# Five projections instead of three in the first pass of a streaming-encoder layer, with the input's squares on ScalarE

## The chip, the cores and the metric

The kernel runs on one core of a Trainium2 chip. The metric is device time in microseconds (us) of one execution. A profiled execution of each kernel gives the trace: what every engine did and when, in us from the first instruction.

## What is computed

One layer of a hybrid encoder over 272 tokens (16 learned ones and 256 of the input) of 2048 channels, in float32:

```python
u = rmsnorm(h, norm_mix)
z = u @ w_in                      # split among three mixers and three gates
y_a = (a_b * causal_dwconv(a_c * a_x, conv_a)) @ w_br_a
y_m = mlstm(...) @ w_br_m         # 4 heads of 256
y_d = diff_attention(...) @ w_br_d  # 4 heads: q, k, v of 128 columns each
h = h + (sig(g_a)*y_a + sig(g_m)*y_m + sig(g_d)*y_d) @ w_out
h = h + channel_mixer(rmsnorm(h, norm_ffn))   # up, conv, GELU gate, down
out = rmsnorm(h, norm_f)[16:]
```

with `rmsnorm(x, g) = x * (mean(x*x) + 1e-6)**-0.5 * g`. What matters here is the first norm and the first projections of `u`, the q, k and v of the differential attention's heads.

## The kernel before, in words

**Layout.** Channels lie on the 128 partitions, tokens along the free dimension. The input is `x_sb`, 16 row blocks of 128 channels by 272 tokens. All weights come as one stream of blocks of 128 by 128, in order of use (`_blocks`, L101); eight blocks are a slab of 512 KB. `Stream` (L152) loads slabs through SP's queue into five buffers (`load_to`, L167) and splits each into two float32r parts (`split_to`, L177): the high part is a cast on ScalarE (L185), the low part a subtraction on VectorE (L186). There are four buffers of split slabs. The first slab goes in two halves.

**Matmuls.** A float32 product is made of three matmuls (`mm3`, L270): high by high (L272), high by low (L273), low by high (L274). A projection of `u` (`proj`, L276) runs over 16 row blocks into one of eight PSUM banks and then defers its evacuation. It covers 258 tokens for q, 272 for k and v.

**Order of the work.** The kernel is written as one program for five engines; the compiler's scheduler places each engine's instructions by priority, mostly in program order. At the first block of each slab the stream splits up to three slabs ahead and calls `tick` (L245), which runs what was deferred with `later(fn, ticks)` once enough ticks are past, in the order in which it was deferred, and advances the background mixers by a step once `HOLD` ticks are past.

**The first pass.** The input is scaled by the norm's gain only; the factor 1/rms of a token (`R`) is applied when a projection is evacuated. Each row block of x is split by `split_scaled` (L298): the high part on ScalarE (L299), the low part on VectorE (L300). The loop at L347 goes through x in steps of `HCH` = 2 row blocks: a load of x and the slabs that this step needs, both on SP's queue, the splits of x, the splits of the slabs, then the squares on GpSimd (L355, L357) and their running sum (L358, L359). `head_jobs` (L478) runs the first `HEAD` = 3 projections (q, k, v of head 0) together, two row blocks of each in turn, so that TensorE can start before all of x is there: 48 blocks, six slabs. The other projections follow one at a time (`job16`, L487).

**The norm.** Eight ticks on, `rstd_cols` (L302) sums the squares over the partitions with six small matmuls (L307), VectorE scales them and GpSimd takes the power -0.5 (L312). One tick later `rstd_rows` (L314) spreads the result over the partitions with diagonal tiles and matmuls (L320, L321) and copies it to `R` (L323). Only then can the first projections be evacuated (`evac_scaled` L394, `v_evac` L425); they hold their banks until then. The first diff-attention steps (`diff_gen`, L434) start after that.

The lines around the change:

```python
HOLD = 9
HEAD, HCH = 3, 2
...
    stream.lead = stream.nraw
    later(lambda: rstd_cols(sqa[:, 0, :], KTILES, rcol), HOLD - 1)
    later(lambda: rstd_rows(KTILES, rcol, R), HOLD)
```

Of the kernel before, what the change touches and what calls it, by code (L numbers as in the profile page):

```python
# [10 lines left out]
F32 = mybir.dt.float32  # L11
F32R = mybir.dt.float32r
AF = mybir.ActivationFunctionType
ALU = mybir.AluOpType
# [10 lines left out]
NH = 4  # L25
# [7 lines left out]
BLK = 8  # L33
HOLD = 9
HEAD, HCH = 3, 2  # projections that share the first pass over the input, and its row blocks per step

# token tiles of the keys (start, size), query tiles (start, size, keys seen)
KTILES = [(0, 16), (16, 128), (144, 128)]
# [7 lines left out]

# ---------------------------------------------------------------- layout of constants and small vectors
def _const_layout():
# [50 lines left out]

# ---------------------------------------------------------------- order in which weight blocks are used  # L100
def _blocks():  # L101
    """(weight, row block, first column) of every block, in order of use"""
    jobs = _jobs()
    out = []
    head, jobs = jobs[:HEAD], jobs[HEAD:]
    for k in range(0, KT, HCH):
        for (name, c0), _, _ in head:
            out += [(name, i, c0) for i in range(k, k + HCH)]
    for (name, c0), k0, K in jobs:
        out += [(name, i, c0) for i in range(k0, k0 + K)]  # L110
    return out
# [40 lines left out]
class Stream:  # L152
    """Weight blocks in order of use: loaded ahead, split into two float32r parts ahead of the matmuls."""

# [48 lines left out]
def encoder_layer_kernel(ctx: ExitStack, tc, xT, wst, wif, vecs, eye, consts, outT):  # L203
# [12 lines left out]

    # ---- small tensors
    vec = base.tile([P, VW], F32, name="vec")
# [5 lines left out]
    warm = base.tile([P, 1], F32, name="warm")  # L224
    S.activation(warm, ones[:, 0:1], AF.Copy, scale=ones[:, 0:1])

# [3 lines left out]

    # ---- deferred work and background mixers, advanced at every slab of weights
    deferred = deque()
# [4 lines left out]
    def later(fn, ticks=0):  # L237
        """run fn at the first tick that is at least so many ticks off, after all that was deferred before"""
        deferred.append((now[0] + 1 + ticks, fn))
# [43 lines left out]
    def proj2(K, xhl, a, b, evac):  # L283
        """as proj, for parts of 256 columns side by side in xhl[:, k, 0 or 1, :]; their sums stay apart"""
        o = bank()
        for k in range(K):
            wh, wl = stream.block()
            one = lambda: T.matmul(o, wh, xhl[:, k, :, a:b], start=(k == 0), stop=(k == K - 1))  # L288
            two = lambda: T.matmul(o[:, : b - a], wl, xhl[:, k, 0, a:b], start=False, stop=False)  # L289
            for f in ((one, two) if k < K - 1 else (two, one)):  # L290
                f()
        later(lambda: evac(o[:, : b - a], o[:, b - a :]))
# [9 lines left out]
    def rstd_cols(acc, cols, out):  # L302
        """out[:, j] = (mean over channels of the squares + eps) ** -0.5 for the tokens of tile j"""
        ps = bank()
        n = len(cols)
        for j, (a, m) in enumerate(cols):
            T.matmul(ps[:m, j : j + 1], acc[:, a : a + m], ones[:, 0:1], start=True, stop=True)  # L307
        ms = small.tile([P, 4], F32, tag="ms", name="ms")
        V.memset(ms, 1.0)
        for j, (a, m) in enumerate(cols):  # L310
            V.tensor_scalar(ms[:m, j : j + 1], ps[:m, j : j + 1], 1.0 / DM, EPS, op0=ALU.mult, op1=ALU.add)
        G.tensor_tensor(out[:, :n], ms[:, :n], nhalf[:, :n], op=ALU.pow)  # L312

    def rstd_rows(cols, r, out):  # L314
        """out[p, t] = rstd of token t, on every partition"""
        ps = bank()
        n = 0
        for j, (a, m) in enumerate(cols):
            dg = small.tile([P, P], F32, tag="dg", name="dg", bufs=2)
            V.tensor_scalar(dg[:m, :m], ident[:m, :m], r[:m, j : j + 1], None, op0=ALU.mult)  # L320
            T.matmul(ps[:, a : a + m], ones[:m, :], dg[:m, :m], start=True, stop=True)  # L321
            n = max(n, a + m)
        V.tensor_copy(out, ps[:, :n])  # L323

    # ---- split of the scaled input and its root mean squares
    x_sb = base.tile([P, KT, TOK], F32, tag="acc", name="x_sb")
# [7 lines left out]
    cst = mix.tile([P, CW], F32, name="cst")  # L334
    sqa = ymp.tile([P, HCH, TOK], F32, tag="y0", name="sqa")
    sq = ymp.tile([P, HCH, TOK], F32, tag="y1", name="sq")
    R = base.tile([P, TOK], F32, name="R")
# [5 lines left out]

    stream.after_load[8] = load_rest
    stream.after_load[12] = lambda: nc.sync.dma_start(cst, consts)
    nc.sync.dma_start(vec[:, :KT], vecs[:, :KT])
    for c in range(0, KT, HCH):  # L347
        nc.sync.dma_start(x_sb[:, c : c + HCH, :], xT[:, c : c + HCH, :])
        stream.load_to(-(-(c + HCH) * HEAD // BLK))
        for k in range(c, c + HCH):  # L350
            split_scaled(uh[:, k, :], ul[:, k, :], x_sb[:, k, :], vs("g_mix", k))
        stream.split_to(-(-(c + HCH) * HEAD // BLK))
        xc = x_sb[:, c : c + HCH, :]
        if c == 0:
            G.tensor_tensor(sqa, xc, xc, op=ALU.mult)  # L355
        else:
            G.tensor_tensor(sq, xc, xc, op=ALU.mult)  # L357
            G.tensor_tensor(sqa, sqa, sq, op=ALU.add)  # L358
    G.tensor_tensor(sqa[:, 0, :], sqa[:, 0, :], sqa[:, 1, :], op=ALU.add)  # L359

    stream.lead = stream.nraw
    later(lambda: rstd_cols(sqa[:, 0, :], KTILES, rcol), HOLD - 1)
    later(lambda: rstd_rows(KTILES, rcol, R), HOLD)

# [3 lines left out]

    # ---- lambda of the differential attention, and scales kept per feature
    lamp = small.tile([P, 64], F32, tag="lamp", name="lamp", bufs=2)  # L370
# [12 lines left out]

    # ---- differential attention
    dqk = ymp.tile([P, NH, TQ + TOK], F32, tag="y0", name="dqk")
# [10 lines left out]
    def token_copy(v3, n, dst, lo=None):  # L396
        """from [token, token tile, ...] in PSUM to SBUF, in two parts if lo is given"""
        for a, b in ((slice(0, 16), slice(0, 1)), (slice(0, P), slice(1, n)))[: 1 if n == 1 else 2]:
            S.copy(dst[a, b], v3[a, b])
            if lo is not None:  # L400
                V.tensor_tensor(lo[a, b], v3[a, b], dst[a, b].bitcast(F32), op=ALU.subtract)

    def transpose_keys(src, nk, nq, dst, lo=None):
        """[query, key] -> [key, key tile, query] in SBUF"""
        ps = bank()
# [9 lines left out]
    def to_tokens(src, dst, lo=None):  # L415
        """dst[token, token tile, feature] from src[feature, token]"""
        ps = bank()
        for j, (k0, m) in enumerate(KTILES):
            T.transpose(ps[:m, j * P : (j + 1) * P], src[:, k0 : k0 + m], ident)
        token_copy(ps[:, 0 : 3 * P].rearrange("p (j q) -> p j q", j=3), 3, dst, lo)  # L420
# [56 lines left out]

    def head_jobs(jobs):  # L478
        ps = [bank() for _ in jobs]
        for k0 in range(0, KT, HCH):  # L480
            for p, (c0, c1, _) in zip(ps, jobs):
                for k in range(k0, k0 + HCH):
                    mm3(p[:, : c1 - c0], uh, ul, k, c0, c1, k == 0, k == KT - 1)
        for p, (c0, c1, evac) in zip(ps, jobs):
            later(lambda p=p, c0=c0, c1=c1, evac=evac: evac(p[:, : c1 - c0]))

    def job16(c0, c1, evac):  # L487
        proj(KT, uh, ul, 0, c0, c1, evac)

    later(lam_setup)  # L490
    for h in range(NH):
        first3 = ((SKIP, TOK, evac_scaled(dq[h], SKIP, TOK)), (0, TOK, evac_scaled(dk[h], 0, TOK)),
                  (0, TOK, v_evac(dv[h])))
        if h == 0:
            head_jobs(first3)
        else:
            for j in first3:
                job16(*j)
        for i in (2, 1, 0):
            later(lambda h=h, i=i: background.append(mark(("d", h, i), diff_gen(h, i))))  # L500

    # ---- gated convolution
    yah = mix.tile([P, 4, TQ], F32R, tag="m0", name="yah")
# [23 lines left out]

    # ---- gates and branch projections
    merged = base.tile([P, KT, TQ], F32, tag="acc", name="merged")
# [20 lines left out]

    # ---- mLSTM: gates of all heads, by token
    wif_raw = mwork.tile([P, KT, 8], F32, tag="ax", name="wif_raw")
# [146 lines left out]

    # ---- last branch, then the output projection of the mixers  # L700
    mh_stack = mstack
# [35 lines left out]

    # ---- channel mixer
    flush(True)
# [62 lines left out]

    # ---- final norm
    rc3 = base.tile([P, 4], F32, name="rc3")
# [58 lines left out]
```

## Time and profile before

| | us |
|---|---|
| median of 3 runs | 1650.77 |
| lowest and highest | 1650.19, 1651.72 |
| span of the profiled execution | 1650.4 |
| TensorE (PE) busy, share of the span | 1626.3, 99% |
| VectorE (DVE) | 1023.9, 62% |
| ScalarE (ACT) | 742.1, 45% |
| GpSimd (POOL) | 72.8, 4% |
| mean granted TensorE clock | 0.995 of full |

The span goes from the first to the last instruction of the profiled execution; that execution has no other time of its own on the page, and its span lies 0.4 us under the median of the runs. PE is TensorE's matmuls, PEld its weight loads, SPq the issuing of DMAs on SyncE. Matmuls are pipelined, so that the durations of consecutive ones overlap: the pace is read from their starts, and a stretch with short gaps can still be shown as busy. A granted clock of 1.00 is 2.4 GHz, of about 0.5 it is 1.2 GHz. In a row, `x2` after a tile's form counts instructions merged into it, and what stands in brackets is how long the engine had been idle before and what ended it.

### The profile page before, as it was taken

What the parts mean: (1) busy time and instruction counts of PE and PEld (TensorE: products, weight loads), DVE (VectorE), ACT (ScalarE), POOL (GpSimd) and SP (SyncE); (2) the same over time, 40 slices, a digit from 0 to 9 for tenths busy, and PEclk for the clock granted to TensorE, in tenths of its full rate; (3) what the DMA queues carried; (4) which work ended last, traced back from release to release, by engine and by line L of the source; (5) the groups of instructions that cost most, each with busy time, mean ns of one, the idle gap of its engine ahead of it and who ended that gap; (6) DMA issues with size and microseconds to landing.
All of it is one profiled execution on the core that took longest, in us unless ns stands there. A gap on an engine that the chain in (4) does not pass through costs nothing.

```text
span 1650.4 us, 29161 instructions
## 1 busy us (share of the span) xinstructions
PE 1626.3 (99%) x11948; PEld 1537.2 (93%) x11948; DVE 1023.9 (62%) x1630; ACT 742.1 (45%) x1082; POOL 72.8 (4%) x76
## 2 busy tenths in 40 slices
PE   7999999999999999999999999999999999999997
PEld 6999999999999999999999999999889999999886
DVE  8556655545555655666666677676555676766554
ACT  4444554344455643444444444444333444444442
POOL 5000000000000000000011000000000000000121
PEclk9999999999999999999999999999999999999998
DMA  6545455444444455555665555555555555555552
GB/s 240 186 156 164 156 166 182 162 142 149 146 154 155 150 181 188 180 182 185 197 203 182 182 188 182 190 179 192 183 188 190 180 190 180 188 184 188 185 188 90
DMA packets 83830, 291.03 MB, mean 176 GB/s; under 512 B 9328, under 2 KB 13808, under 8 KB 83568
## 3 DMA queue, kind: packets, MB, share of 16 engines
q1 hardware_dynamic: 82592, 288.18, 53.7%
q8 instruction: 93, 1.52, 0.4%
q10 hardware_dynamic: 1104, 0.98, 0.2%
q14 instruction: 41, 0.34, 0.1%
HBM read 287.03 MB, written 2.10 MB: 175 GB/s over the span
## 4 chain that ended last, share of the span: by engine, by line
PE 97%; DVE 1%; DMA 1%; issue 1%; POOL 0%; SPq 0%; POOLq 0%; ACT 0%; DVEq 0%; ACTq 0%
PE ps L272 22%; PE ps L273 21%; PE ps L274 21%; PE ps L288 20%; PE ps L289 10%; PE ps L464 1%; DMA w_raw<-in_wst 1%; PE ps L624 0%; PE ps L645 0%; PE ps L409 0%; DVE uhl L300 0%; PE ps L443 0%; DMA x_sb<-in_xT 0%; PE ps L621 0%; DVE h L819 0%
## 5 line engine op out<-in xcount | busy, mean ns | idle before, releaser
L185 ACT CAST w_hi<-w_raw 128x1024 fp32r<-128x1024 f32 (+1 forms) x537 | 562.8, 1048 | 813.8 <-issue 316.0
L186 DVE TENSOR_TENSOR w_lo<-w_raw,w_hi 128x1024 fp32r<-128x1024 f32 (+1 forms) x537 | 660.2, 1230 | 416.0 <-ACT w_hi L185 410.0
L272 PE MATMUL ps<-uhl,w_hi 128*128 128x258 f32 (+2 forms) x1664 | 486.1, 292 | 6.3 <-ACT w_hi L185 6.3
L273 PE MATMUL ps<-uhl,w_hi 128*128 128x258 f32 (+2 forms) x1664 | 477.4, 287 | 1.9 <-DVE uhl L300 1.9
L274 PE MATMUL ps<-uhl,w_lo 128*128 128x258 f32 (+2 forms) x1664 | 474.6, 285 | 4.2 <-DVE w_lo L186 4.2
L272 PEld LDWEIGHTS ps<-uhl,w_hi 128*128 128x128 f32 x1664 | 315.3, 190 | 10.9 <-ACT w_hi L185 6.3
L274 PEld LDWEIGHTS ps<-uhl,w_lo 128*128 128x128 f32 x1664 | 315.5, 190 | 5.2 <-DVE w_lo L186 5.2
L273 PEld LDWEIGHTS ps<-uhl,w_hi 128*128 128x128 f32 x1664 | 316.6, 190 | 3.1 <-DVE uhl L300 3.0
L288 PE MATMUL ps<-fhl,w_hi 128*128 128x512 f32 x704 | 252.3, 398 | 0.0
L288 PE MATMUL ps<-act,w_hi 128*128 128x512 f32 x682 | 237.5, 394 | 0.0
L273 PE MATMUL ps<-fhl,w_hi 128*128 128x258 f32 x704 | 199.8, 284 | 0.0
L272 PE MATMUL ps<-fhl,w_hi 128*128 128x258 f32 x704 | 198.8, 282 | 0.0
L274 PE MATMUL ps<-fhl,w_lo 128*128 128x258 f32 x704 | 197.5, 281 | 0.0
L289 PE MATMUL ps<-fhl,w_lo 128*128 128x256 f32 x704 | 190.0, 280 | 0.0
L289 PE MATMUL ps<-act,w_lo 128*128 128x256 f32 x682 | 187.6, 282 | 0.0
L288 PEld LDWEIGHTS ps<-fhl,w_hi 128*128 128x128 f32 x704 | 132.4, 188 | 28.3
L288 PEld LDWEIGHTS ps<-act,w_hi 128*128 128x128 f32 x682 | 126.1, 188 | 26.8
L273 PEld LDWEIGHTS ps<-fhl,w_hi 128*128 128x128 f32 x704 | 133.2, 189 | 2.1
L289 PEld LDWEIGHTS ps<-fhl,w_lo 128*128 128x128 f32 x704 | 133.2, 189 | 1.8
L274 PEld LDWEIGHTS ps<-fhl,w_lo 128*128 128x128 f32 x704 | 134.3, 191 | 0.0
L272 PEld LDWEIGHTS ps<-fhl,w_hi 128*128 128x128 f32 x704 | 132.4, 188 | 0.0
L289 PEld LDWEIGHTS ps<-act,w_lo 128*128 128x128 f32 x682 | 128.3, 188 | 3.0
(222 smaller groups left out, 1599.9 us busy)
## 6 DMA issues: line engine op xcount, KB each, us to landing
w_raw<-in_wst SPq DMA_DIRECT2D x535, 512.0 KB, 3.4
x_sb<-in_xT SPq DMA_DIRECT2D x8, 272.0 KB, 7.4
xr<-in_xT SPq DMA_DIRECT2D x16, 129.0 KB, 3.1
cst<-in_consts SPq DMA_DIRECT2D x1, 1252.5 KB, 9.3
out<-h SPq DMA_DIRECT2D x4, 256.0 KB, 3.1
out<-h ACTq DMA_DIRECT2D x3, 256.0 KB, 3.3
w_raw<-in_wst SPq DMA_DIRECT2D x2, 256.0 KB, 3.8
vec<-in_vecs SPq DMA_DIRECT2D x1, 246.5 KB, 4.4
```

What stands on the lines that cost most here:

```text
L185: self.nc.scalar.copy(hi[:, a], raw[:, a])
L186: self.nc.vector.tensor_tensor(lo[:, a], raw[:, a], hi.bitcast(F32)[:, a], op=ALU.subtract)
L272: T.matmul(o, wh, xh[:, k, c0:c1], start=start, stop=False)
L273: T.matmul(o, wh, xl[:, k, c0:c1], start=False, stop=False)
L274: T.matmul(o, wl, xh[:, k, c0:c1], start=False, stop=stop)
L288: one = lambda: T.matmul(o, wh, xhl[:, k, :, a:b], start=(k == 0), stop=(k == K - 1))
L289: two = lambda: T.matmul(o[:, : b - a], wl, xhl[:, k, 0, a:b], start=False, stop=False)
L464: T.matmul(ps[:nq, :P], aT[:m, j, :nq], dv[h][:m, j, :], start=(j == 0), stop=(j == n - 1))
```

## The change

The first pass takes five projections instead of three (q, k, v of head 0, q and k of head 1): 80 blocks, ten slabs. Its steps are one, one and then two row blocks at a time. x of the first two steps is loaded through ScalarE's queue, ahead of the warm-up activation; the x of later steps is issued on SP's queue two steps ahead. The squares are taken on ScalarE, in place over x, one step behind the splits; VectorE adds them up in four instructions, deferred to tick 10; `rstd_cols` and `rstd_rows` come at ticks 12 and 13. The remaining vectors, the identity and the constant tables are loaded behind slabs 11 and 14 instead of 8 and 12. The matmuls of every projection stay the same, in another order.

```diff
-HOLD = 9
-HEAD, HCH = 3, 2
+HOLD = 13
+HEAD = 5
+STEPS = [(0, 1), (1, 1), (2, 2), (4, 2), (6, 2), (8, 2), (10, 2), (12, 2), (14, 2)]
...
-    for k in range(0, KT, HCH):
+    for k, n in STEPS:
         for (name, c0), _, _ in head:
-            out += [(name, i, c0) for i in range(k, k + HCH)]
+            out += [(name, i, c0) for i in range(k, k + n)]
...
     warm = base.tile([P, 1], F32, name="warm")
-    S.activation(warm, ones[:, 0:1], AF.Copy, scale=ones[:, 0:1])
...
-    sqa = ymp.tile([P, HCH, TOK], F32, tag="y0", name="sqa")
-    sq = ymp.tile([P, HCH, TOK], F32, tag="y1", name="sq")
+    sqa = ymp.tile([P, TOK], F32, tag="y0", name="sqa")
...
-    stream.after_load[8] = load_rest
-    stream.after_load[12] = lambda: nc.sync.dma_start(cst, consts)
+    stream.after_load[11] = load_rest
+    stream.after_load[14] = lambda: nc.sync.dma_start(cst, consts)
+
+    def load_x(q, c, n):
+        q.dma_start(x_sb[:, c : c + n, :], xT[:, c : c + n, :])
+
+    def square(c, n):
+        S.activation(x_sb[:, c : c + n, :], x_sb[:, c : c + n, :], AF.Square)
+
     nc.sync.dma_start(vec[:, :KT], vecs[:, :KT])
-    for c in range(0, KT, HCH):
-        nc.sync.dma_start(x_sb[:, c : c + HCH, :], xT[:, c : c + HCH, :])
-        stream.load_to(-(-(c + HCH) * HEAD // BLK))
-        for k in range(c, c + HCH):
+    load_x(S, *STEPS[0])
+    load_x(S, *STEPS[1])
+    S.activation(warm, ones[:, 0:1], AF.Copy, scale=ones[:, 0:1])
+    for n, (c, w) in enumerate(STEPS):
+        if n + 2 < len(STEPS):
+            load_x(nc.sync, *STEPS[n + 2])
+        slabs = -(-(c + w) * HEAD // BLK)
+        stream.load_to(slabs)
+        for k in range(c, c + w):
             split_scaled(uh[:, k, :], ul[:, k, :], x_sb[:, k, :], vs("g_mix", k))
-        stream.split_to(-(-(c + HCH) * HEAD // BLK))
-        xc = x_sb[:, c : c + HCH, :]
-        if c == 0:
-            G.tensor_tensor(sqa, xc, xc, op=ALU.mult)
-        else:
-            G.tensor_tensor(sq, xc, xc, op=ALU.mult)
-            G.tensor_tensor(sqa, sqa, sq, op=ALU.add)
-    G.tensor_tensor(sqa[:, 0, :], sqa[:, 0, :], sqa[:, 1, :], op=ALU.add)
+        stream.split_to(slabs)
+        if n:
+            square(*STEPS[n - 1])
+    square(*STEPS[-1])
+
+    def square_sums():
+        for n in (8, 4, 2, 1):
+            dst = x_sb[:, 0:n, :] if n > 1 else sqa.unsqueeze(1)
+            V.tensor_tensor(dst, x_sb[:, 0:n, :], x_sb[:, n : 2 * n, :], op=ALU.add)
 
     stream.lead = stream.nraw
-    later(lambda: rstd_cols(sqa[:, 0, :], KTILES, rcol), HOLD - 1)
-    later(lambda: rstd_rows(KTILES, rcol, R), HOLD)
+    later(square_sums, HOLD - 4)
+    later(lambda: rstd_cols(sqa, KTILES, rcol), HOLD - 2)
+    later(lambda: rstd_rows(KTILES, rcol, R), HOLD - 1)
...
-    def head_jobs(jobs):
+    def head_jobs(jobs, then):
         ps = [bank() for _ in jobs]
-        for k0 in range(0, KT, HCH):
+        for k0, n in STEPS:
             for p, (c0, c1, _) in zip(ps, jobs):
-                for k in range(k0, k0 + HCH):
+                for k in range(k0, k0 + n):
                     mm3(p[:, : c1 - c0], uh, ul, k, c0, c1, k == 0, k == KT - 1)
-        for p, (c0, c1, evac) in zip(ps, jobs):
+        for n, (p, (c0, c1, evac)) in enumerate(zip(ps, jobs)):
             later(lambda p=p, c0=c0, c1=c1, evac=evac: evac(p[:, : c1 - c0]))
+            then(n)
...
+    head_jobs(parts[:HEAD], start_heads)
+    for n in range(HEAD, len(parts)):
+        job16(*parts[n])
+        start_heads(n)
```

`parts` lists q, k, v of the four heads in the order in which they ran before; `start_heads` starts the background steps of a head after its v, as before.

## Rows read from the trace of the kernel before

**Rows 1.** The page, part 1: busy us, share of the span and instructions of TensorE.

```profile
PE 1626.3 (99%) x11948; PEld 1537.2 (93%) x11948; DVE 1023.9 (62%) x1630; ACT 742.1 (45%) x1082; POOL 72.8 (4%) x76
```

**Rows 2.** Busy time by stretches, 0 to 43.42 us; columns in the first row.

```profile
core 0: us, PE busy (x) PEld busy (x) DVE busy (x) ACT busy (x) POOL busy (x), PEclk, DMA share, GB/s
0.00:6.27 6.27, 0.00 (x0) 0.00 (x0) 1.17 (x7) 3.07 (x6) 1.30 (x5) 1.00 0.63 198
6.27:10.27 4.00, 4.00 (x16) 3.77 (x17) 3.66 (x5) 2.15 (x4) 2.55 (x2) 1.00 0.99 368
10.27:17.10 6.83, 5.20 (x35) 4.32 (x34) 6.75 (x5) 6.54 (x12) 6.46 (x5) 1.00 1.04 412
17.10:20.43 3.33, 1.51 (x9) 1.09 (x9) 3.33 (x4) 2.94 (x6) 3.17 (x3) 1.00 0.74 262
20.43:23.90 3.47, 3.47 (x16) 3.47 (x16) 3.47 (x3) 0.24 (x1) 3.31 (x3) 0.52 0.02 8
23.90:34.20 10.30, 7.71 (x45) 7.08 (x45) 10.30 (x10) 1.85 (x2) 6.63 (x5) 0.83 0.44 141
34.20:43.42 9.22, 9.22 (x77) 9.17 (x75) 5.84 (x13) 3.35 (x4) 0.00 (x0) 1.00 0.86 298
```

**Rows 3.** Timeline of TensorE's matmuls: start us, duration us, what.

```profile
22.75 0.43 PE L274 MATMUL ps<-uhl,w_lo 128*128 128x272 f32 x1
22.97 0.43 PE L272 MATMUL ps<-uhl,w_hi 128*128 128x272 f32 x1
...
41.00 0.29 PE L273 MATMUL ps<-uhl,w_hi 128*128 128x258 f32 x1
...
43.30 0.28 PE L274 MATMUL ps<-uhl,w_lo 128*128 128x258 f32 x1
43.52 0.74 PE L307 MATMUL ps<-ones,sqa 128*16 128x1 f32 x6
...
44.33 0.29 PE L273 MATMUL ps<-uhl,w_hi 128*128 128x272 f32 x1
...
47.10 0.29 PE L274 MATMUL ps<-uhl,w_lo 128*128 128x272 f32 x1
```

**Rows 4.** VectorE's groups by line and shape, 5 to 30 us: busy us, mean ns | idle.

```profile
L300 DVE SCALAR_TENSOR_TENSOR uhl<-x_sb,vec,uhl 128x272 fp32r<-128x272 f32 x12 | 14.9, 1287 | 4.6 <-ACT uhl L299 4.6
L186 DVE TENSOR_TENSOR w_lo<-w_raw,w_hi 128x1024 fp32r<-128x1024 f32 x4 | 8.8, 2201 | 0.1
```

**Rows 5.** Timeline of VectorE after GpSimd's last sum.

```profile
32.61 0.90 DVE L300 SCALAR_TENSOR_TENSOR uhl<-x_sb,vec,uhl 128x272 fp32r<-128x272 f32 x2
33.44 1.21 DVE L186 TENSOR_TENSOR w_lo<-w_raw,w_hi 128x1024 fp32r<-128x1024 f32 x1
```

**Rows 6.** Timeline of ScalarE, 0 to 10 us.

```profile
0.73 1.28 ACT L225 ACT_TABLE_LOAD   x1 [0.73 <-PEq L852]
...
4.78 0.93 ACT L299 ACTIVATE uhl<-x_sb,vec 128x272 fp32r<-128x272 f32 x2 [2.46 <-DMA x_sb<-in_xT]
5.62 1.12 ACT L185 CAST w_hi<-w_raw 128x512 fp32r<-128x512 f32 x2
...
9.52 1.05 ACT L185 CAST w_hi<-w_raw 128x1024 fp32r<-128x1024 f32 x1 [1.04 <-DMA w_raw<-in_wst]
```

**Rows 7.** Timeline of ScalarE near the end: a Square (L788) and a scaled Copy (L793).

```profile
1637.65 0.42 ACT L788 ACTIVATE sq<-h 128x256 f32<-128x256 f32 x1 [6.41 <-DVE h L781]
1638.10 0.51 ACT L793 ACTIVATE h<-h,vec 128x256 f32<-128x256 f32 x1
```

**Rows 8.** Timeline of SP's issuing: the first load of x.

```profile
1.19 0.42 SPq L348 DMA_DIRECT2D x_sb<-in_xT  x1
```

**Rows 9.** Timeline of VectorE: an early add, R, and the first evacuations.

```profile
37.32 0.15 DVE L562 TENSOR_TENSOR eye<-ident 16x8 f32<-16x8 f32 x1
...
48.64 0.44 DVE L323 COPY R<-ps 128x272 f32<-128x272 f32 x1 [0.60 <-PE ps L321]
...
50.12 0.77 DVE L394 TENSOR_TENSOR dqk<-ps,R 128x258 f32<-128x258 f32 x2
```

More of the change, by code (lines that the diff above doesn't have):

```diff
@@ L490, in encoder_layer_kernel, with start_heads @@
     later(lam_setup)
[L491 to L500, printed above, removed]
+    parts = [part for h in range(NH) for part in (
+        (SKIP, TOK, evac_scaled(dq[h], SKIP, TOK)), (0, TOK, evac_scaled(dk[h], 0, TOK)), (0, TOK, v_evac(dv[h])))]
+    def start_heads(n):
+        if n % 3 == 2:
+            for i in (2, 1, 0):
+                later(lambda h=n // 3, i=i: background.append(mark(("d", h, i), diff_gen(h, i))))
+    head_jobs(parts[:HEAD], start_heads)
+    for n in range(HEAD, len(parts)):
+        job16(*parts[n])
+        start_heads(n)
     yah = mix.tile([P, 4, TQ], F32R, tag="m0", name="yah")
```

## The prediction, made before the changed kernel was run

> **What bounds the kernel now.** I read the page's busy shares first. TensorE's matmuls cover 1626.3 of 1650.4 us [rows 1], so only the remaining 24 us, and stretches in which TensorE runs at its lower clock, can be won without removing matmuls. The change removes none: it orders 240 of them otherwise. So I looked for the lost time by stretches [rows 2]. Nothing runs on TensorE before 6.27; in 10.27 to 20.43 it is busy for 5.20 of 6.83 and then 1.51 of 3.33 us; after that its clock falls to 0.52 of full, which is the 1.2 GHz level, although it is then busy throughout. Only from 34.2 on is it both busy and at 2.4 GHz. The place to count is the end of slab 7, the last matmul before the six of L307 at 43.52 [rows 3].
>
> At full clock 22 steps of 272 columns take 47.10 - 44.33 = 2.77 us, 0.126 each, and 19 of 258 columns take 43.30 - 41.00 = 2.30, 0.121 each; at the low level one takes 22.97 - 22.75 = 0.22 [rows 3]. A slab (8 blocks, 24 matmuls) is thus 2.98 us, with 0.124 as the mean. Eight slabs are 192 matmuls: 96 of either width in this stretch, 23.7 us of work. They end at 43.30 + 0.12 = 43.4. **19.7 us are lost before that point**; nothing later can gain, as TensorE's rows stay full there.
>
> Who withholds the work? VectorE is busy for all of 10.27 to 34.2, beside GpSimd with 6.46 of 6.83 and 3.17 of 3.33 us [rows 2]. While GpSimd squares, the low half of one row block (L300) takes 1.29 and that of a slab (L186) 2.20 us; after GpSimd's last sum, 0.45 (0.90 for two) and 1.21 [rows 4, 5]. Per row block before, VectorE needs 1.29 + 3/8 x 2.20 = 2.1 us, for 9 matmuls of 1.1 us. So TensorE is starved by VectorE, and VectorE is slow beside GpSimd.
>
> **The parts and their cost.**
>
> *Squares off GpSimd.* GpSimd loses its 16 instructions of the first pass; nothing else waits there but one pow per norm. VectorE's price falls to 1.21 per slab and 0.45 per row block.
>
> *Five projections.* One row block now carries 15 matmuls, 1.86 us, for 5/8 slab; a slab has 1.6 row blocks. Per slab of 2.98 us of TensorE, VectorE needs 1.21 + 1.6 x 0.45 = 1.93. ScalarE needs 1.05 for the cast, 1.6 x 0.47 for the splits [rows 6], and the squares: 0.42 for 256 columns [rows 7] is the dear end, 0.42 x 1.6 = 0.67; two blocks in one instruction can only save fixed cost. Sum 2.47. DMA: 512 + 1.6 x 136 KB = 730 KB, 1.8 us at 412 GB/s [rows 2]. TensorE is the longest of the four, so once fed it stays fed. The slots of split slabs give a lead of three slabs, 8.9 us, of which cast and low half use 2.3.
>
> *The start.* This sets what remains lost. Slab 1 is the first whole slab; its cast waited for its DMA until 9.52 [rows 6]. Ahead of it lay, itself included, 8 + 272 + 512 + 272 + 512 = 1576 KB (sizes from the shapes). In the new order another 272 KB, row blocks 4 and 5, are issued ahead. At 368 GB/s [rows 2] that is 0.75 us: 10.3. The ends: 9.5, if the ScalarE queue's early start makes up for it, and 10.7, if all of the time since 2.5 us stretches in proportion. I take 10.3, since the row of this stretch prices the bytes. Cast 1.05 and low half 1.21 give 12.6. TensorE can by then have done slab 0 and two matmuls, 26 x 0.124 = 3.2 us. Loss 9.4. The splits of row blocks 2 and 3 stand behind slab 1's cast on ScalarE; two of 0.47, two low halves of 0.45 and one cast end at 13.5, when TensorE reaches that block: 0 to 0.4, I take 0.2. **Loss after: 9.6.**
>
> Is TensorE's own start hidden by that? x of row blocks 0 and 1 goes out on ScalarE's queue. ScalarE then sits idle for 2.46 us before its first split [rows 6]; two issues of about 0.42 [rows 8] and the table load of 1.28 moved behind them fit into that. SP loses one issue of 0.42 ahead of slab 0. Slab 0's first half had landed by 5.62; 272 KB more ahead of it put it at 6.4 at worst, its cast ends at 7.0. From 7.0, all 24 matmuls at the low level take 5.3 us: 12.3, before 12.6. So a later start costs nothing, and half-size first loads gain nothing, as long as slab 1 is the last to come. The Trainium skill, DMA: Bandwidth & Descriptors, "Issuing engines are not separate DMA queues", says that issuing from another engine saves issue time only, since all share 16 DMA engines. By that the move would be worth 0.4 us at the first split; by the sum above, nothing.
>
> *Sums on VectorE.* Four adds over 8, 4, 2 and 1 row blocks: 15 x 272 = 4080 columns at 1.21/1024 [rows 5], 4.8 us, queued from tick 10 ahead of slab 13's low half. VectorE has 1.7 us free per slab and the lead has 6.6 to spare: cost 0. If they run only behind slab 12's low half, they end 1.3 us after TensorE reaches L307 (slab 11): a stall of 0 to 1.3. I take 0, since VectorE's order shows work moved forward when it is ready: L562's add, of a later stage, ran at 37.32 [rows 9].
>
> *R and the banks.* Five head banks, two further projections and the sums fill all 8 banks until R is there. From L307 to R took 48.64 + 0.44 - 43.52 = 5.6 us, to the first evacuation's end 7.0 [rows 3, 9]. After: slab 11 starts at 9.6 + 11 x 2.98 = 42.4, the first bank is free at 49.4, and the projection at slab 14 wants it at 51.3. 1.9 us to spare: cost 0; each us beyond costs one. The start of the background mixers three ticks later is hidden by their slack. The identity and the masks are loaded behind slabs 11 and 14 while TensorE is at slab 2 and 5: far ahead.
>
> **Sum**: 19.7 - 9.6 = 10.1 us less. The profiled span is 1650.4; the median of the runs is 1650.77, 0.4 above it. 1650.8 - 10.1 = **1640.7**.
>
> **Rivals.** A difference under 0.2% (3.3 us: below 1647.5 or above 1654.1 counts as a change) can't be told from none here.
>
> 1. *The clock falls once more.* It fell after 1.51 busy in 3.33 us and stood at 0.52 for 3.47 [rows 2]. The wait for slab 1 leaves a hole of about 1 us at 11.6 to 12.6. One fall costs 3.47 x (1 - 0.124/0.22) = 1.5; with slab 1 at 10.7, 0.4 more: 1642.6; with two falls 1644.1. Against it: 10.27 to 17.1 had a hole share of 1.63 in 6.83 and kept the clock. Chance 0.2.
>
> 2. *R comes late and TensorE stands with all banks taken.* Sums late by 1.3 and the evacuations behind a low half or two (1.21 each): 1.3 + 2.4 - 1.9 = 1.8, plus the stall of 1.3 at L307: 1643.8. Against: the low halves run slabs ahead. Chance 0.07.
>
> 3. *VectorE is slow for another cause* (the weights' DMA). Then 2.20 + 1.6 x 1.29 = 4.3 per slab against 2.98: slab 9's low half comes at 10.3 + 1.05 + 2.20 + 8 x 4.3 = 48, with its matmuls 51; 240 matmuls are 29.8, the loss 21: 1652, no change. Against: L300 at 0.45 and L186 at 1.21 at 32.6 to 34.7 [rows 5], DMA then at work as well. Chance 0.04.
>
> 4. *Slower: Square and Copy switch ScalarE's table.* Each of the nine Squares would bring a load of 1.28 [rows 6] there and one back: 23 us. ScalarE's first pass is 16 x 0.47 + 10 x 1.05 + 16 x 0.42 = 24.7, with loads 48, from about 4: 52; a low half and the last slab later 56. Loss 56 - 29.8 = 26: 1657. It decides from 1.85 us per Square on, where the loss reaches 19.7. Against: at 1637.65 a Square is followed by a scaled Copy at 1638.10, no load between [rows 7]. The Trainium skill, ScalarE: Activation LUTs, "Table sets: the hidden batching unit", speaks for it: calls are to be batched by set, and its list of functions in every set names copy, not square. The trace disagrees. Chance 0.03.
>
> The case without any hole, slab 1 at 9.5, gives 8.6 lost: 1639.7; an earlier clock and start might take another 1 us.
>
> **Numbers.** Forecast 0.66, own range 1639 to 1642.5; rivals as above. The range that leaves out 3, 4 and the ends of the others: 1638.6 to 1645.0. Faster by over 0.2%: forecast, 1, 2 less a little, 0.9; same 0.06; slower 0.04.
>
> **What the next profile should show.** L300 at about 0.45 and L186 at 1.21 in the first 40 us; no GpSimd instruction there but the pow; TensorE full from about 13 us on, at full clock; slab 1's cast near 10.3; no table load between Square and Copy; L307 near 42.4 without idle time ahead. I am wrong if TensorE still waits for L300 or L186 after 14 us, if it waits for a bank near 51, or if the clock is low after 15.

## The result, and the profile after

The changed kernel takes 1642.56 us (median of 4 runs, 1642.14 to 1642.94) against 1651.24 of the kernel before in the same runs; the ratio is 0.9947, 95% interval 0.9935 to 0.9959. That is 8.7 us less; 1640.7 had been forecast, with 1638.6 to 1645.0 as the range. The median lies just above the narrower range of 1639 to 1642.5, which had been given 0.66. The spans of the two profiled executions are 1650.4 and 1640.7 us, 9.7 apart.

The busy time by stretches of the changed kernel, to be held against [rows 2] (start and end in us, length, then busy time and instructions of each engine, granted clock, DMA share, GB/s):

```profile
6.27:10.27 4.00, 2.79 (x12) 2.78 (x13) 3.33 (x7) 3.86 (x10) 0.00 (x0) 1.00 1.02 399
10.27:17.10 6.83, 6.83 (x53) 6.82 (x53) 5.38 (x8) 6.83 (x13) 0.00 (x0) 1.00 1.03 407
17.10:20.43 3.33, 3.33 (x29) 3.33 (x28) 2.82 (x5) 3.33 (x7) 0.00 (x0) 1.00 1.07 412
20.43:23.90 3.47, 3.47 (x30) 3.47 (x29) 3.17 (x4) 3.27 (x5) 0.00 (x0) 1.00 0.76 262
23.90:34.20 10.30, 10.30 (x85) 10.30 (x84) 9.56 (x13) 4.75 (x6) 0.00 (x0) 1.00 0.80 277
```

From its start at 7.49 on TensorE is full, where before it was busy for 5.20 of 6.83 and 1.51 of 3.33 us, and the clock does not fall again: 30 matmuls fit into 20.43 to 23.90, where 16 did. GpSimd is empty.

What TensorE waited for in the first 60 us, first before, then after (who waited for whom: us in total, times, longest):

```profile
PE ps L272 <- ACT w_hi L185: 6.3, 1, 6.3
PE ps L274 <- DVE w_lo L186: 4.2, 4, 1.5
PE ps L273 <- DVE uhl L300: 1.9, 3, 0.9
```

```profile
PE ps L272 <- ACT w_hi L186: 7.5, 1, 7.5
```

Both waits for VectorE are gone; only the start is left, and it is later. (Lines of the changed kernel have other numbers: the cast is L186 there, the low half L187, the Square L350, the sums L371.) VectorE's groups from 5 to 30 us, to be held against [rows 4] (busy us, mean ns | idle):

```profile
L187 DVE TENSOR_TENSOR w_lo<-w_raw,w_hi 128x1024 fp32r<-128x1024 f32 x9 | 10.9, 1223 | 2.3 <-ACT w_hi L186 2.3
L300 DVE SCALAR_TENSOR_TENSOR uhl<-x_sb,vec,uhl 128x272 fp32r<-128x272 f32 x15 | 6.9, 496 | 1.9 <-ACT uhl L299 1.8
L371 DVE TENSOR_TENSOR x_sb<-x_sb 128x2176 f32<-128x2176 f32 x1 | 2.4, 2418 | 0.0
```

The low half of a slab went from 2.20 to 1.22 us, that of a row block from 1.29 to 0.50 (two in a row overlap and take 0.91). ScalarE's timeline at the start, to be held against [rows 6]:

```profile
1.66 1.28 ACT L355 ACT_TABLE_LOAD   x1 [1.66 <-PEq L869]
...
3.15 0.51 ACT L299 ACTIVATE uhl<-x_sb,vec 128x272 fp32r<-128x272 f32 x1
5.46 0.93 ACT L299 ACTIVATE uhl<-x_sb,vec 128x272 fp32r<-128x272 f32 x2 [1.80 <-DMA x_sb<-in_xT]
...
6.81 1.27 ACT L186 CAST w_hi<-w_raw 128x512 fp32r<-128x512 f32 x2
...
9.56 0.64 ACT L350 ACTIVATE x_sb<-x_sb 128x544 f32<-128x544 f32 x1
10.11 1.03 ACT L186 CAST w_hi<-w_raw 128x1024 fp32r<-128x1024 f32 x1
11.04 0.94 ACT L299 ACTIVATE uhl<-x_sb,vec 128x272 fp32r<-128x272 f32 x2
```

The first cast starts at 6.81 instead of 5.62, slab 1's at 10.11. Square, cast and scaled Copy follow each other without a table load. TensorE starts at 7.49 and reaches the norm at 42.17 (timeline of TensorE's matmuls; before in [rows 3]):

```profile
7.49 0.58 PE L272 MATMUL ps<-uhl,w_hi 128*128 128x258 f32 x1 [7.49 <-ACT w_hi L186]
...
42.17 0.74 PE L307 MATMUL ps<-ones,sqa 128*16 128x1 f32 x6
```

Eleven slabs lie before that point: 96 matmuls at 0.121 and 168 at 0.126, 32.8 us. They end at about 42.1, so **9.3 us are lost, against 19.7 before**. The start is 7.5 of that. The rest is the pace of the low level, 0.22 us from one start to the next: the first 16 matmuls take until 11.25, 1.8 us more than 16 x 0.124.

### The profile page after: what moved, and what is told of

Its sections match the earlier page's. It is cut to its first block, busy times and chain, and to the rows that moved or that the text cites. A ratio compares the mean times of both kernels' runs of the same rounds, so it can differ in the third digit from the quotient of the medians.

```text
span 1640.7 us, 29157 instructions
## 1 busy us (share of the span) xinstructions
PE 1621.1 (99%) x11948; PEld 1533.9 (93%) x11948; DVE 1014.6 (62%) x1634; ACT 748.6 (46%) x1093; POOL 49.6 (3%) x60
## 3 DMA queue, kind: packets, MB, share of 16 engines
q10 hardware_dynamic: 1392, 1.26, 0.2%
## 4 chain that ended last, share of the span: by engine, by line
PE 98%; issue 1%; DVE 0%; DMA 0%; ACT 0%; POOL 0%; SPq 0%; POOLq 0%; DVEq 0%; ACTq 0%
PE ps L272 22%; PE ps L273 21%; PE ps L274 21%; PE ps L288 20%; PE ps L289 10%; PE ps L477 1%; PE ps L641 0%; PE ps L662 0%; PE ps L422 0%; DMA w_raw<-in_wst 0%; PE ps L456 0%; PE ps L638 0%; DVE h L836 0%; PE ps L432 0%; PE ps L664 0%
## 5 line engine op out<-in xcount | busy, mean ns | idle before, releaser
L186 ACT CAST w_hi<-w_raw 128x1024 fp32r<-128x1024 f32 (+1 forms) x537 | 562.7, 1048 | 804.9 <-issue 310.5
L187 DVE TENSOR_TENSOR w_lo<-w_raw,w_hi 128x1024 fp32r<-128x1024 f32 (+1 forms) x537 | 656.3, 1222 | 417.2 <-ACT w_hi L186 413.0
```

Source lines behind the costliest of these rows:

```text
L186: self.nc.scalar.copy(hi[:, a], raw[:, a])
L187: self.nc.vector.tensor_tensor(lo[:, a], raw[:, a], hi.bitcast(F32)[:, a], op=ALU.subtract)
```

## The experiments

**Which of the two parts brings it?** First, squares and running sum back on GpSimd, all else of the change kept:

```diff
-        if n:
-            square(*STEPS[n - 1])
-    square(*STEPS[-1])
+        xc = x_sb[:, c : c + w, :]
+        if n < 2:
+            G.tensor_tensor(sqa[:, n : n + 1, :], xc, xc, op=ALU.mult)
+        else:
+            G.tensor_tensor(sq, xc, xc, op=ALU.mult)
+            G.tensor_tensor(sqa, sqa, sq, op=ALU.add)
```

> Five projections and all else of the change stay; the squares and their running sum go back to GpSimd. Theory (VectorE is slowed by GpSimd, and that starved TensorE): L300 near 1.3 us and the low half of a slab near 2.2 us until GpSimd's last sum, VectorE needs 2.2 + 1.6 x 1.3 = 4.3 us per slab against 2.98 us of TensorE, so TensorE waits for VectorE again in slabs 1 to 9 and the time is 1650 to 1654 us, about that of the kernel before. Rival (more matmuls per row block were what mattered): TensorE stays fed, 1642 to 1644 us.

Measured: 1651.6 us against 1650.76 before, ratio 1.0003 (0.9993 to 1.0012). Waits of TensorE and VectorE's groups:

```profile
PE ps L272 <- ACT w_hi L186: 7.8, 1, 7.8
PE ps L274 <- DVE w_lo L187: 6.6, 5, 2.4
```

```profile
L300 DVE SCALAR_TENSOR_TENSOR uhl<-x_sb,vec,uhl 128x272 fp32r<-128x272 f32 x11 | 14.3, 1341 | 2.3 <-ACT uhl L299 2.3
L187 DVE TENSOR_TENSOR w_lo<-w_raw,w_hi 128x1024 fp32r<-128x1024 f32 x4 | 7.8, 1947 | 0.0
```

The whole gain is gone, and the waits for VectorE are back: five projections, with the new steps and loads, bring nothing while the squares stay on GpSimd.

Second, the reverse: three projections, squares on ScalarE, the new steps and loads kept:

```diff
-HOLD = 13
-HEAD = 5
+HOLD = 10
+HEAD = 3
```

> Squares stay on ScalarE and their sums on VectorE; the first pass takes three projections instead of five (HOLD 10). Theory (the move of the squares carries most of the gain): VectorE needs 0.45 + 3/8 x 1.21 = 0.90 us per row block and ScalarE 0.47 + 3/8 x 1.05 + 0.32 = 1.18, against 1.12 of TensorE, so TensorE is starved only a little: 1643 to 1645.5 us. Rival (five projections are needed for it, since three give TensorE too little work for what each row block costs the other engines and the DMA): 1647 us or more, with TensorE short of work between 12 and 25 us and its clock falling.

Measured: 1642.41 us, ratio 0.9948 (0.9934 to 0.9963), the same as the change. TensorE starts at 7.35 and is full from then on, but for 0.2 us at L307. The move of the squares carries all of the measurable gain; five projections, the edit that the change names first, add nothing that the time shows. In the traces five stand 0.7 us ahead at the second norm (878.74 against 879.44; with three the pace of 0.22 us lasts to 13.3 instead of 11.2), and the last four matmuls give 0.5 of it back. No run moves the squares alone, with the steps and loads of the kernel before.

**Does ScalarE matter, or only GpSimd's absence?** The squares on VectorE itself:

```diff
-        S.activation(x_sb[:, c : c + n, :], x_sb[:, c : c + n, :], AF.Square)
+        V.tensor_tensor(x_sb[:, c : c + n, :], x_sb[:, c : c + n, :], x_sb[:, c : c + n, :], op=ALU.mult)
```

> The changed kernel with the squares on VectorE (products in place) instead of ScalarE; the sums stay. Theory (it matters that GpSimd reads nothing, not which of the other two engines squares): VectorE needs 1.21 + 1.6 x (0.45 + 0.33) = 2.5 us per slab against 2.98 of TensorE, so TensorE stays fed and the time is 1642 to 1643.5 us. Rival (ScalarE is what the move needs, since VectorE was the engine short of time): TensorE waits for L300 or the low half in slabs 1 to 9, 1645 us or more.

Measured: 1642.87 us, ratio 0.9948 (0.9933 to 0.9963). The squares among VectorE's groups, and TensorE's waits in the first 60 us:

```profile
L350 DVE TENSOR_TENSOR x_sb<-x_sb 128x544 f32<-128x544 f32 x7 | 4.9, 716 | 0.0
```

```profile
PE ps L272 <- ACT w_hi L186: 7.7, 1, 7.7
```

VectorE, the engine that was short of time, does the squares as well (0.72 us for two row blocks) and is still fast enough: TensorE waits for its start alone.

**How does GpSimd slow VectorE?** Three kernels add work on GpSimd to the changed kernel, over constants, into a tile `dm` that nothing else reads:

```diff
+    dm = ymp.tile([P, 3, 512], F32, tag="y1", name="dm")
+    V.memset(dm[:, 0:2, :], 0.0)
+    for _ in range(18):
+        G.tensor_tensor(dm[:, 2, :], dm[:, 0, :], dm[:, 1, :], op=ALU.mult)
```

> The changed kernel, with 18 products of 512 columns added on GpSimd from the start on, over two constant operands and into a tile that nobody reads. Theory (GpSimd's reads slow VectorE, whatever the data): while GpSimd runs, L300 near 1.3 and the low half of a slab near 2.2 us, TensorE waits for VectorE, the time is 4 to 10 us above the changed kernel. Rival (VectorE was slowed by x being read by two engines, or by the DMA): L300 and the low half stay at 0.45 and 1.22 us, the time within 1 us of the changed kernel.

```diff
...
+    for _ in range(36):
+        G.tensor_tensor(dm[:, 2, :256], dm[:, 0, :256], dm[:, 1, :256], op=ALU.mult)
```

> The changed kernel with 36 products of 256 columns added on GpSimd instead of 18 of 512: the same work in instructions half as long. Beside products of 512 columns a VectorE instruction took about 1.05 us more whatever its own length (1.45 for 0.45, 1.75 for 0.68, 2.30 for 1.22). Theory (a VectorE instruction waits for one whole GpSimd instruction, then runs at full speed): the addition halves to 0.5 to 0.65 us, and VectorE's need per slab falls from about 4.6 to 1.8 + 1.6 x 1.0 = 3.4 us against 2.98 of TensorE: 1643 to 1648 us. Rival (the two engines share a bandwidth): the addition stays near 1 us and grows with VectorE's own length, 1652 us or more.

```diff
...
+    for _ in range(18):
+        G.memset(dm, 0.0)
```

> The changed kernel with 18 memsets of 1536 columns added on GpSimd from the start on, in place of products: GpSimd writes but reads no operand. Theory (VectorE waits for GpSimd instructions that read): L300 and the low half stay at 0.45 and 1.22 us, the time stays within 1 us of the changed kernel's 1642.6. Rival (any GpSimd instruction that is at work in the memory holds VectorE up): both longer by 0.5 to 1.1 us, 1648 us or more.

Measured: 1653.1 us with products of 512 columns (ratio to the kernel before 1.0016, 1.0007 to 1.0026), 1648.15 with products of 256 (0.9978, 0.9969 to 0.9988), 1642.67 with the memsets (0.9948, 0.9932 to 0.9965). VectorE's groups from 5 to 30 us, 512 columns first, then 256, then the memsets:

```profile
L300 DVE SCALAR_TENSOR_TENSOR uhl<-x_sb,vec,uhl 128x272 fp32r<-128x272 f32 x12 | 17.0, 1454 | 2.0 <-ACT uhl L299 2.0
L187 DVE TENSOR_TENSOR w_lo<-w_raw,w_hi 128x1024 fp32r<-128x1024 f32 x3 | 6.9, 2297 | 0.0
L187 DVE TENSOR_TENSOR w_lo<-w_raw,w_hi 128x512 fp32r<-128x512 f32 x2 | 3.4, 1755 | 0.0
```

```profile
L300 DVE SCALAR_TENSOR_TENSOR uhl<-x_sb,vec,uhl 128x272 fp32r<-128x272 f32 x13 | 12.1, 976 | 2.2 <-ACT uhl L299 2.2
L187 DVE TENSOR_TENSOR w_lo<-w_raw,w_hi 128x1024 fp32r<-128x1024 f32 x6 | 10.5, 1744 | 0.0
L187 DVE TENSOR_TENSOR w_lo<-w_raw,w_hi 128x512 fp32r<-128x512 f32 x2 | 2.4, 1213 | 0.0
```

```profile
L187 DVE TENSOR_TENSOR w_lo<-w_raw,w_hi 128x1024 fp32r<-128x1024 f32 x9 | 10.9, 1224 | 2.3 <-ACT w_hi L186 2.3
L300 DVE SCALAR_TENSOR_TENSOR uhl<-x_sb,vec,uhl 128x272 fp32r<-128x272 f32 x15 | 6.9, 497 | 1.6 <-ACT uhl L299 1.6
```

and GpSimd's own groups with the memsets and with the products of 256 columns, then the first product of 512 and the first of 256 columns, while VectorE has nothing to do (timeline):

```profile
L354 POOL MEMSET dm<- 128x1536 f32 x18 | 24.9, 1382 | 1.3 <-POOLq L872 0.3
```

```profile
L355 POOL TENSOR_TENSOR dm<-dm 128x256 f32<-128x256 f32 x36 | 40.5, 1126 | 4.5 <-DVE ms L309 1.7
```

```profile
2.16 1.26 POOL L355 TENSOR_TENSOR dm<-dm 128x512 f32<-128x512 f32 x1 [1.72 <-DVE ms L309]
```

```profile
2.16 0.72 POOL L355 TENSOR_TENSOR dm<-dm 128x256 f32<-128x256 f32 x1 [1.72 <-DVE ms L309]
```

Against the changed kernel (0.50, 1.22, and 0.69 for the half slab) the long products add 0.96, 1.07 and 1.06 us to a VectorE instruction, the short ones 0.48, 0.52 and 0.52. The addition hardly depends on VectorE's own length; it halves when GpSimd's instruction has half the columns. Undisturbed, GpSimd needs 1.26 us for the long product and 0.72 for the short one, 0.2 more than they add. So the times fit a VectorE that does not run slower, but stands at each instruction for most of one GpSimd instruction. GpSimd loses too: its short product takes 1.13 us on average, against 0.72 undisturbed. Memsets of 1.38 us, 25 us of them in all, add nothing. The Trainium skill, SBUF — State Buffer, "Who interferes with whom", describes this: the port pair that the two engines share is an exclusive lock, and a VectorE instruction with two inputs in SBUF contends with a GpSimd instruction that reads SBUF, not with one that only writes it. The traces agree, with the additions above. Only products, with two operands, and memsets, with none, were tried.

**What is still lost?** The slabs issued ahead of x of two steps later:

```diff
-        if n + 2 < len(STEPS):
-            load_x(nc.sync, *STEPS[n + 2])
         slabs = -(-(c + w) * HEAD // BLK)
         stream.load_to(slabs)
+        if n + 2 < len(STEPS):
+            load_x(nc.sync, *STEPS[n + 2])
```

> In each step of the first pass the slabs are issued on SP's queue before x of two steps ahead, not after it. Theory (TensorE's start is set by the arrival of slab 0, behind 272 KB of x that is not needed yet): the first cast starts near 6.1 instead of 6.81 us, TensorE starts near 6.8 instead of 7.49, the matmul at L307 comes 0.5 to 0.8 us earlier than 42.24, 1641.5 to 1642.5 us. Rival (slab 1 is as late as before, and a start that comes earlier only waits there): L307 within 0.2 us of 42.24.

Measured: 1641.81 us, ratio 0.9946 (0.9929 to 0.9962). The first cast starts at 5.92, TensorE at 6.57, slab 1's cast at 9.33, L307 at 41.21, 1.0 us earlier. The critical chain (start us, us, what) of the changed kernel, then of this one:

```profile
1.65 5.14 DMA w_raw<-in_wst
6.81 0.63 ACT w_hi L186
```

```profile
1.18 4.29 DMA x_sb<-in_xT
5.49 0.52 ACT uhl L299
```

In the changed kernel the arrival of slab 0's first half at 6.79 sets the start, and the bytes ahead of it delay it. With the slabs first, x of row block 1 sets it: it comes through ScalarE's queue at 5.47, and its split stands ahead of the cast on ScalarE. Taken further, to the order of need:

```diff
-        n = 2 if i == 0 else 1
+        n = 4 if i == 0 else 1
...
-    load_x(S, *STEPS[1])
...
-        if n + 2 < len(STEPS):
-            load_x(nc.sync, *STEPS[n + 2])
         slabs = -(-(c + w) * HEAD // BLK)
         stream.load_to(slabs)
+        if n + 1 < len(STEPS):
+            load_x(nc.sync, *STEPS[n + 1])
```

> The changed kernel with the first slab in four pieces, x of row block 1 on SP's queue, and each step's slabs issued before x of the next step: all loads in order of need. Theory (what is lost now is the arrival of slab 0, the start at the low clock and the arrival of slab 1, all set by bytes that are issued too early): TensorE starts at 4.8 to 5.8 us, slab 1's cast near 8.5 instead of 10.11, L307 at 40.0 to 41.0 instead of 42.24, 1640.3 to 1641.5 us. Rival (fixed latency of a DMA and the splits set the start, not bytes): start not before 6.3 us and L307 not before 41.1, no better than with the weights first (1641.8).

Measured: **1640.09 us** against 1651.66 before in the same runs, ratio 0.9933 (0.9918 to 0.9948), better than both kernels: its slowest run took 1640.62, the fastest of the changed kernel 1642.14. TensorE starts at 4.18:

```profile
4.18 0.58 PE L272 MATMUL ps<-uhl,w_hi 128*128 128x258 f32 x1 [4.18 <-ACT w_hi L186]
...
39.98 0.74 PE L307 MATMUL ps<-ones,sqa 128*16 128x1 f32 x6
```

Slab 1's cast came at 8.40, L307 at 39.98: 7.1 us lost. Two thirds of the 3.3 us by which the start is earlier arrive, 2.2; the rest goes to the low clock, whose pace of 0.22 lasts until 10.3, for 27 matmuls instead of 16. So I gave TensorE work ahead of its weights:

```diff
+    wps = bank()
+    for _ in range(5):
+        T.matmul(wps[:, :P], ones, ones, start=True, stop=True)
```

> The kernel with all loads in order of need, with five 128-column products of a constant tile issued on TensorE from 1 us on, into a bank that nobody reads, so that it is at work before its first weights come at 4.18 us. Theory (part of what is still lost is the low clock from 4.18 to 10.3 us, in which 27 matmuls take 0.1 us each too long): the clock rises near 7, 1.0 to 2.0 us are gained against 1640.1, L307 at 38.0 to 39.0 instead of 39.98. Rival (the arrival of slab 1 and its low half holds TensorE up instead, or the clock rises when it did): L307 within 0.4 us of 39.98.

Measured: 1640.68 us, ratio 0.9934 (0.9918 to 0.9951): no gain. Here the steps of TensorE became short at 8.2, but in this execution the first weights came later (start at 4.96), and TensorE then stood at slab 1: it waited for its cast before the matmul of 9.91. L307 came at 40.42. Slab 1 holds the earlier clock up; that part of the rival stands. What the earlier clock is worth with weights as early as in the run before is not shown.

Last, three projections again, now with the loads in order of need (`HEAD = 3`, `HOLD = 10`), and the same with `HOLD = 13`:

> The kernel with all loads in order of need (1640.1), with three projections in the first pass instead of five (HOLD 10). Theory (five projections bring nothing measurable, since with VectorE unhindered three keep TensorE fed as well): 1639.5 to 1641.5 us, TensorE without a wait after its start. Rival (with an earlier start TensorE outruns the loads at 1.12 us per row block, and five projections cover that): TensorE waits between 6 and 14 us, 1642 us or more.

> All loads in order of need and three projections, as the run that took 1646.7 us, but with HOLD 13 in place of 10, so that the sums of squares have three ticks more. In that run TensorE waited 2.6 us at L307 for the sums and 1.6 us for row block 1, and its clock fell after it. Theory (the loss of 6.6 us against five projections came from the norm's place, and three projections feed TensorE as well): no wait at L307, 1640 to 1642.5 us. Rival (three projections give TensorE too little work per row block once it starts early): waits elsewhere in the first 40 us in its place, 1644 us or more.

Measured: 1646.66 us (ratio 0.9972, 0.9962 to 0.9982) and 1641.95 (0.9945, 0.9928 to 0.9961). TensorE's waits, HOLD 10 first:

```profile
PE ps L272 <- ACT w_hi L186: 4.1, 1, 4.1
PE ps L307 <- DVE sqa L370: 2.6, 1, 2.6
PE ps L272 <- ACT uhl L299: 1.6, 1, 1.6
```

```profile
PE ps L272 <- ACT w_hi L186: 4.1, 1, 4.1
PE ps L272 <- ACT uhl L299: 1.2, 1, 1.2
```

With HOLD 10 the norm's matmuls come too soon after the first pass and wait for the sums; the granted clock stood at 0.81 of full from 34.2 to 43.4, the stretch of that wait (L307 comes at 36.0). With HOLD 13 that is gone, and 1.9 us remain against five projections (1641.95 against 1640.09). There five projections have a use: three give TensorE too little work in step 0, so it waits 1.2 us for row block 1. My theory for the first of these two runs was wrong, that for the second right but for this rest.

## Why the prediction was right, point by point

**What bounds the kernel** held: VectorE, slowed by GpSimd, starved TensorE. Without GpSimd's reads VectorE's prices were those of [rows 5], and the 19.7 us lost shrank to 9.3, where 9.6 had been worked out.

**Squares off GpSimd** was right, and is the whole of what the time shows. The Square of two row blocks took 0.64 us, under the bound of 0.84. **Five projections** was the step that I credited wrongly. I made one sum for both edits and never asked what three would do. With VectorE at 0.45 + 3/8 x 1.21 = 0.90 us per row block against 1.12 of TensorE, VectorE has time enough for three; ScalarE at 1.18 would be a little short, yet the second run shows no wait for it. The total was right, its attribution was not.

**The start** was mis-sized: 7.0 at worst had been given for TensorE's start, it was 7.49, as slab 0's first half landed at 6.79 and not at 6.4. Slab 1's cast came at 10.11 instead of 10.3 and its low half ended at 12.40. TensorE's first matmul with that half began at 12.49, so start and slab 1 bind at almost the same time; "a later start costs nothing" held by 0.1 us only. The run with the slabs first had both earlier, the start by 0.9 and slab 1's cast by 0.8 us, and does not tell them apart. The hole that I expected at 11.6 to 12.6 did not open, and with it the first rival (the clock falls once more) had no ground.

**The sums** cost nothing, as taken: they ran from 25.06 to 33.7, long before L307. **R and the banks** too: R was there 47.28 + 0.44 - 42.17 = 5.55 us after L307, and the first evacuations followed (timeline of VectorE; before in [rows 9]):

```profile
47.28 0.44 DVE L323 COPY R<-ps 128x272 f32<-128x272 f32 x1 [0.59 <-PE ps L321]
...
48.77 0.77 DVE L407 TENSOR_TENSOR dqk<-ps,R 128x258 f32<-128x258 f32 x2
```

The rival of a VectorE slow for another cause fell too: its low half of a slab took 1.22 us with the DMA share at 1.02 to 1.07. So did that of table loads: none stands between Square, cast and scaled Copy.

**From the sum to the time.** I set the span of the profiled execution 0.4 us under a run's time. The later runs list both, and the time is 1.7 to 1.9 us above the span in all of them (1642.45 and 1640.7 for the profiled execution after). The one before, at a span of 1650.4, was thus one of about 1652.2; runs of the kernel before scatter from 1650.08 to 1652.75, with spans of 1648.3 to 1650.9. The sum took its loss from the slow end of that scatter and was subtracted from the median: 1652.2 - 10.1 = 1642.1 would have been the consistent forecast. The loss itself shrank by 19.7 - 9.3 = 10.4, and the traces keep that distance to the end: the second norm's first matmul and those of the last norm stand 10.35 us apart (before, then after):

```profile
889.09 0.72 PE L307 MATMUL ps<-ones,acc 128*128 128x1 f32 x6
1638.37 0.36 PE L808 MATMUL ps<-ones,acc 128*128 128x1 f32 x2
1640.41 0.68 PE L815 MATMUL ps<-dg,ones 128*128 128x128 f32 x4 [1.46 <-DVE dg L814]
```

```profile
878.74 0.73 PE L307 MATMUL ps<-ones,acc 128*128 128x1 f32 x6
1628.02 0.36 PE L825 MATMUL ps<-ones,acc 128*128 128x1 f32 x2
1630.06 1.20 PE L832 MATMUL ps<-dg,ones 128*128 128x128 f32 x4 [1.45 <-DVE dg L831]
```

0.5 us of it is given back by the last four matmuls, 1.20 instead of 0.68 us. In the other eleven profiles they took between 0.68 and 1.20 us; what decides it was not tried.

## What to carry to other kernels

When VectorE looks overloaded, first compare the duration of its instructions in stretches with and without GpSimd at work. Here about half of its busy time from 5 to 30 us (13.4 of 25.0) was what the same instructions took beyond their length without GpSimd, and taking GpSimd's products away brought the whole gain, the rebalancing beside it none. Where several edits come together, price each alone. Once the supply is right, look at the start for bytes issued before they are needed: loads in order of need took 9.3 us of loss to 7.1 here, as long as each arriving piece brought enough work.

## What was not expected of the hardware

The addition to a VectorE instruction beside GpSimd's products is a fixed one (about 1.0 us beside products of 512 columns, 0.5 beside 256), so short VectorE instructions suffer most: a row block's low half took 1.45 us for 0.50. And the granted clock reads 1.00 for 6.27 to 10.27 us while matmuls step at 0.22 us, the pace that goes with 0.52 in [rows 2, 3]: after a start the pace of the starts showed the clock here, the column did not.
